# An RWKV-7 core with 16 x 16 inverses, a series of 64 x 64 matmuls and one head on each half of the partitions

## The chip, the core and the metric

The kernel runs on one core of one Trainium2 chip. The metric is the device time of one execution in microseconds (us); lower is better. PE is the matmul engine, PEld its weight loads, DVE the vector engine, ACT the scalar engine, POOL GpSimd, SP the engine that issues the DMAs.

## What is computed

A trunk of two layers on 512 tokens of 1024 channels, in float32. Each layer normalises x, projects it, runs four groups of heads in parallel (a bidirectional Mamba-2 SSD, a bidirectional RWKV-7, differential attention, grouped attention), multiplies the joined outputs by w_out, normalises and adds to x. The change is in the RWKV-7 part. Its core is this scan, for 8 heads of 64 channels and for each of two directions:

```
def step(S, inp):
    r_t, w_t, k_t, v_t, a_t, b_t = inp
    sa = jnp.einsum("bhvk,bhk->bhv", S, a_t)
    S = S * w_t[:, :, None, :] + sa[..., None] * b_t[:, :, None, :] + v_t[..., None] * k_t[:, :, None, :]
    return S, jnp.einsum("bhvk,bhk->bhv", S, r_t)
```

S is a 64 x 64 state. Around it stand token shifts, low-rank decays, a group norm, a bonus term and a gate.

## The kernel before, in words

The scan is computed in chunks of 64 tokens, 8 chunks per direction d, for four pairs j of heads (e is the head in the pair). That makes 32 units (d, e, chunk) per pair. `rwkv` (line 252) runs for each pair:

- **prep** (322): all that needs no product of two tokens. It is done for pair j + 1 while pair j is in work, in small steps that `Ahead` (485) hands out.
- **products** (429) and **turned** (443): b and k against a and r of each chunk (tile AT, through PSUM tile pa), and b, k and v turned so that tokens stand on partitions (BKT; v goes into the upper half of UV).
- **the solver** (519 to 543): each unit needs the inverse of a 64 x 64 unit triangular matrix. DVE turns its two 32 x 32 diagonal blocks to one matrix per partition, on 64 partitions, and inverts them by 31 steps of forward substitution, a multiplication (541, tile ot) and an addition (543, written under the name UV) per step.
- **the merge** (544 to 564): three DVE transposes, 64 matmuls of 32 x 32 (tile pr) for the blocks off the diagonal, and copies into TT, the transposed inverses.
- **the chain** (566 to 618): for 8 chunks in turn, for both directions: products of the state and v (bk, shown as ch), copy to Xs (588), times TT, two copies into UV (591), times BKT, four operations for the new state (606 or 609), and the outputs (tile yb). POOL makes the decayed state Sl (598).

`Filler` (1072) weaves the projections of the next pair (pjc) and the attention (pjt, sc, ptp, ob and others) in between: `fill(F_SV)` after a solver step or `fill(F_CH)` after a chunk releases that many us of its work, scaled so that all of END * 299.5 us is released over the four pairs. A weight is loaded by DMA, split by ACT into a rounded part whi (143) and by POOL into the rest wlo (144), and each product is three matmuls. The framework then orders the instructions of each engine by its own priorities, and every engine works its list in order.

Of the kernel before, what the change touches and what calls it, by code (L numbers as in the profile page):

```python
# [10 lines left out]
F32 = mybir.dt.float32  # L11
F32R = mybir.dt.float32r
# [25 lines left out]
N_SV = 2  # L38
N_CH = 2
C_LAG = 2  # L40
# [6 lines left out]
# columns of the constant array  # L47
# [5 lines left out]
C_BK = C_ONE + 2  # L53
# [4 lines left out]
C_N = C_NHALF + 16  # L58
# kept apart: the masks and chunk starts of the SSD, the rotary tables (cos and sin; 1-D and row positions by token tile)
# [3 lines left out]
# rounded to float32r on the chip, which changes none of them  # L63
# [3 lines left out]
C_ALL = C_E + 16  # L67
# [9 lines left out]
def trunk(ctx: ExitStack, tc: tile.TileContext, x_in, win, wwd, wdt, wout, w2a, cols, rows, sscal, consts, out, dbg=None,  # L77
# [14 lines left out]
    # the activation table comes in while the first loads run  # L92
# [17 lines left out]
    bkcol = cst[:, C_BK:C_BK + 1]  # L110
    nhalf = cst[:, C_NHALF:C_NHALF + 16]
    cr = cpool.tile([128, 272], F32R, name="cr")
# [36 lines left out]
    def pre_norm(xt, tt, lay, pool, pspool, tag):  # L149
        """RMSNorm of one 128-token tile and its transposed, split copy."""  # L150
# [14 lines left out]
    def load_layer(i):  # L165
# [7 lines left out]
        # 1 - mu, w0/2, a0/2, k_a/2, 1 - k_a/2  # L173
# [12 lines left out]
    def proj_cm(i, g, ps, consume):  # L186
        """Two 128-column tiles of the projection, channels on partitions."""
# [14 lines left out]
    def low_rank(pw, ws, tt):  # L202
        """The RWKV's low-rank inputs of two token tiles, channels on partitions."""
# [10 lines left out]
    def proj_early(i, g, ps, consume):  # L214
        """256 columns of the projection, one token tile after another."""
# [16 lines left out]
    def proj_tm(i, g, ps, consume):  # L232
        """256 columns of the projection, tokens on partitions; two token tiles to a bank."""
# [17 lines left out]
    # ------------------------------------------------------------------ RWKV-7  # L251
    def rwkv(i, lay, pw, ps, rp, fill):
        c, dv = lay["cols"], lay["dv"]

        def lerp(raw, n, d, dst):
            """raw + (neighbour - raw) * mu; the backward direction runs in reversed time."""
# [22 lines left out]
        def block_mm(o, m, src):  # L279
            """m @ src for a matrix that float32r holds exactly."""  # L280
# [7 lines left out]
        # states of the two heads of a pair, each in its own block  # L288
        Sbuf = [[rp.tile([128, 2, 64], F32, tag=f"S{d}{n}", name=f"S{d}{n}") for n in range(2)] for d in range(2)]
        for d in range(2):  # L290
            for n in range(2):
                G.memset(Sbuf[d][n], 0.0)

        # a of the pair in work, r of two pairs
        AR = rp.tile([128, 3, 2, 8, 64], F32, tag="AR", name="AR")
# [26 lines left out]
        def prep(j):  # L322
            """Everything of a head pair that needs no product of two of its tokens; yields now and then."""
# [5 lines left out]
            s["a"], s["r"] = Aa, Ar = AR[:, 0], AR[:, 1 + j % 2]  # L329
# [11 lines left out]
            for d in range(2):  # L341
# [19 lines left out]
                # max(sum, 1e-24) as relu(sum - 1e-24) + 1e-24  # L361
# [21 lines left out]
                BK = rp.tile([128, 8, 2, 64], F32, tag="BK", name="BK", bufs=2)  # L383
                s["BK"].append(BK)
# [9 lines left out]
                V.tensor_tensor(BK[:, :, 0, :], v3(b1), il, op=ALU.mult)  # L394
# [33 lines left out]

        def products(j, c0, n):
            """n chunks of AT."""  # L430
            ar = AR[:, 0:2 + j % 2:1 + j % 2]
            for d in range(2):
                BK = sts[j]["BK"][d]
                for e in range(2):
                    hp = slice(64 * e, 64 * e + 64)
                    pa = ps.tile([128, n, 128], F32, tag="g", name="pa")
                    for cc in range(n):
                        mm(pa[:, cc, :].rearrange("p (a t) -> p a t", a=2), BK[hp, c0 + cc].rearrange("p a t -> p (a t)"),
                           ar[hp, :, d, c0 + cc, :], True, True)
                    V.tensor_tensor(AT[:, d, e, c0:c0 + n].rearrange("p c a t -> p c (a t)"), pa,  # L440
                                    rmask.unsqueeze(1).to_broadcast([128, n, 128]), op=ALU.mult)

        def turned(j):
            BK, v = sts[j]["BK"], sts[j]["v"]
            for d in range(2):
                for e in range(2):
# [956 lines left out]
```

## Time and profile before

| | |
|---|---|
| median of 3 runs | 1897.48 us (1895.22 to 1897.68) |
| span of the profiled execution, the one time that the profile gives of it | 1898.5 us |
| busy share of PE / PEld / DVE / ACT / POOL | 89% / 71% / 72% / 44% / 41% |
| four head pairs of layer 1, from the first solver to the last chain | 117.4 to 703.8 us |
| the same of layer 2 | 1056.4 to 1648.9 us |

Busy is the time in which an engine has an instruction in work; matmuls overlap, so a busy PE is not a PE at its peak. PEclk in a row of windows is the granted share of the 2.4 GHz clock, at each moment 1.0 or 0.5 (1.2 GHz). A wait names who waits, for whom, the total, how often and the longest.

### The profile page before, as it was taken

To read this page: it belongs to the slowest core of one execution; us is meant where nothing else is said; L and a number is where in the kernel's file an instruction comes from. 1 tells how busy PE (TensorE), PEld (TensorE's weight loads), DVE (VectorE), ACT (ScalarE), POOL (GpSimd) and SP (SyncE) were. 2 spreads that over 40 slices of the span, in tenths; PEclk is the share of its full clock that TensorE was granted. 3 is DMA by queue.
4 is the path that set the end of the run, shared out by engine and by line. 5 is a ranking of instruction groups with operands and counts; after the bars stand their busy time and mean duration, and the time that the engine had idled before them with its cause. 6 is when DMAs were issued, how large, how long until landed. Compare 5 with 4: busy or idle time off the path is not lost.

```text
span 1898.5 us, 28978 instructions
## 1 busy us (share of the span) xinstructions
PE 1683.3 (89%) x10744; PEld 1340.6 (71%) x10744; DVE 1363.0 (72%) x2946; ACT 838.4 (44%) x1606; POOL 782.7 (41%) x826
## 2 busy tenths in 40 slices
PE   7898988897988898988898899889989888989888
PEld 6576776676776776876775777666767767767666
DVE  4577789779868657886246877887797795588752
ACT  4643345435525245443345442553454252455432
POOL 4433445424542334443455333443444433344433
PEclk9877899898989899989998778998988898999899
DMA  4211111011111114223431111110111111142223
GB/s 147 58 39 43 28 29 51 32 34 40 40 40 30 33 40 137 70 68 93 129 105 49 38 28 32 34 45 31 34 45 28 40 34 35 34 134 62 89 78 117
DMA packets 57485, 107.91 MB, mean 57 GB/s; under 512 B 6784, under 2 KB 8832, under 8 KB 57344
## 3 DMA queue, kind: packets, MB, share of 16 engines
q1 hardware_dynamic: 57344, 106.07, 18.7%
q8 instruction: 84, 1.38, 0.3%
q14 instruction: 57, 0.47, 0.1%
HBM read 95.56 MB, written 10.49 MB: 56 GB/s over the span
## 4 chain that ended last, share of the span: by engine, by line
PE 46%; DVE 36%; POOL 6%; ACT 6%; issue 5%; DMA 2%; POOLq 0%; SPq 0%; ACTq 0%; DVEq 0%
PE pjt L83 9%; PE mix L83 6%; PE pjc L83 5%; PE ch L83 5%; DVE UV L543 5%; DVE ot L541 4%; PE pa L83 4%; PE yb L83 3%; PE sc L83 3%; PE p L83 2%; PE ob L83 2%; POOL wlo L144 2%; DVE As L528 2%; DVE nm L845 1%; PE pr L83 1%
## 5 line engine op out<-in xcount | busy, mean ns | idle before, releaser
L144 POOL TENSOR_TENSOR wlo<-wf,whi 128x512 fp32r<-128x512 f32 x228 | 338.9, 1492 | 334.1 <-ACT whi L143 293.3
L83 PE MATMUL pjt<-whi,hhi 128*128 128x256 f32 x960 | 297.8, 311 | 13.3 <-DVE gate L315 6.9
L83 PE MATMUL pjt<-wlo,hhi 128*128 128x256 f32 x960 | 295.4, 309 | 8.4 <-POOL wlo L144 8.4
L83 PE MATMUL pjt<-whi,hlo 128*128 128x256 f32 x960 | 294.6, 307 | 0.0
L143 ACT ACTIVATE whi<-wf 128x512 fp32r<-128x512 f32 x228 | 141.2, 627 | 226.9 <-PE pjt L83 109.0
L83 PEld LDWEIGHTS pjt<-whi,hhi 128*128 128x128 f32 x960 | 196.1, 204 | 29.9 <-issue 8.1
L83 PEld LDWEIGHTS pjt<-wlo,hhi 128*128 128x128 f32 x960 | 195.4, 204 | 17.3 <-POOL wlo L144 9.0
L83 PEld LDWEIGHTS pjt<-whi,hlo 128*128 128x128 f32 x960 | 195.7, 204 | 8.9 <-issue 5.3
L83 PE MATMUL pjc<-hhi,whi 128*128 128x512 f32 x384 | 165.0, 431 | 11.5 <-ACT raw L269 5.2
L83 PE MATMUL pjc<-hhi,wlo 128*128 128x512 f32 x384 | 163.6, 427 | 0.0
L83 PE MATMUL pjc<-hlo,whi 128*128 128x512 f32 x384 | 162.4, 423 | 0.0
L598 POOL TENSOR_SCALAR Sl<-S,lamC,cst 128x128 f32<-128x128 f32 x96 | 47.1, 491 | 248.0 <-DVE S L606 168.1
L83 PE MATMUL sc<-qT,qT 64*128 64x512 f32 (+1 forms) x256 | 108.3, 519 | 21.6 <-ACT p L848 11.6
L541 DVE TENSOR_TENSOR ot<-As,UV 64x31 f32<-64x31 f32 (+15 forms) x248 | 123.7, 499 | 5.0
L543 DVE TENSOR_TENSOR UV<-UV,ot 64x31 f32<-64x31 f32 (+15 forms) x248 | 121.3, 489 | 5.2
L848 ACT ACTIVATE p<-sc,nm 128x512 f32<-128x512 f32 x96 | 65.7, 685 | 108.0 <-DVE nm L845 107.7
L83 PE MATMUL mix<-whi,ylo 128*128 128x512 f32 x256 | 106.1, 414 | 5.5 <-DVE ylo L1189 5.5
L83 PE MATMUL mix<-wlo,yhi 128*128 128x512 f32 x256 | 104.6, 409 | 0.0
L83 PEld LDWEIGHTS pjc<-hhi,whi 128*128 128x128 f32 x384 | 77.9, 203 | 33.9 <-ACT raw L269 6.8
L83 PE MATMUL mix<-whi,yhi 128*128 128x512 f32 x256 | 99.7, 411 | 1.9 <-ACT yhi L1188 1.9
L606 DVE SCALAR_TENSOR_TENSOR UV<-ch,lamC,Sl 64x64 f32<-64x64 f32 x192 | 54.0, 281 | 58.7 <-PE ch L83 35.4
L845 DVE TENSOR_REDUCE nm<-sc 128x1 f32<-128x512 f32 x96 | 65.6, 683 | 38.4 <-PE sc L83 37.7
(316 smaller groups left out, 4013.0 us busy)
## 6 DMA issues: line engine op xcount, KB each, us to landing
wf<-in_win_dram SPq DMA_DIRECT2D x224, 256.0 KB, 2.9
wf<-in_wout_dram SPq DMA_DIRECT2D x64, 256.0 KB, 2.6
y<-y_dram SPq DMA_DIRECT2D x24, 256.0 KB, 3.2
xt<-in_x_dram SPq DMA_DIRECT2D x8, 512.0 KB, 4.0
y_dram<-y SPq DMA_DIRECT2D x16, 256.0 KB, 2.0
y_dram<-rs SPq DMA_DIRECT2D x8, 256.0 KB, 2.8
x_dram<-t SPq DMA_DIRECT2D x8, 256.0 KB, 2.2
xt<-x_dram SPq DMA_DIRECT2D x4, 512.0 KB, 3.7
```

The lines of the kernel that those rows point to most:

```text
L83: PE.matmul(o, lhsT, rhs, start=start, stop=stop, skip_group_check=skip)
L143: S.activation(hi, wf, AF.Copy)
L144: G.tensor_tensor(lo, wf, hi.bitcast(F32), op=ALU.subtract)
L528: V.transpose(out=As[hp], in_=ATu[hp, :, 0, hp].rearrange(swap))
L541: V.tensor_tensor(o3, As[:, jj + 1:32, jj:jj + 1].to_broadcast([64, n, jj + 1]), Ti[:, jj:jj + 1, 0:jj + 1].to_broadcast([64, n, jj + 1]), ...
L543: V.tensor_tensor(Ti[:, jj + 1:32, 0:jj + 1], Ti[:, jj + 1:32, 0:jj + 1], o3, op=ALU.add)
L598: G.tensor_scalar(Sl, St[d], lamC[:, d, cc:cc + 1], zero, op0=ALU.mult, op1=ALU.add)
L606: V.scalar_tensor_tensor(dst, bk[hp, 128:192], lc, Sl[hp, e, :], op0=ALU.mult, op1=ALU.add)
L845: V.tensor_reduce(nm, sc, axis=AX, op=ALU.max, negate=True)
L848: S.activation(p, sc, AF.Exp, bias=nm, accum_out=sm)
```

## The change

- The diagonal blocks are 16 x 16. DVE turns all four quarters of the partitions, folds the two halves of each 32 x 32 transpose into one matrix per partition on 128 partitions, and needs 15 steps instead of 31. Eight transposes write the inverses back, as DN and, transposed, DT.
- The rest of each 64 x 64 inverse comes from a series: Mp is the part off the diagonal blocks times DN, and three rounds compute TT = DT + Mp TT by matmuls (PSUM tiles ch). POOL masks the blocks and clears DT and DN.
- Head e stands on partitions 64 e to 64 e + 63. Almost every matmul of the core is 64 x 64, one for each head, on that half of the rows and of the columns. A pair has 464 of them (before 218 of other shapes); each shows as two PE instructions, as before.
- Products with v leave the chain: px, pk and py are made for all chunks at once, and the bank yb and py are first written by a matmul with a zero weight. The chain has three matmul steps per chunk with a DVE operation behind each; the decayed state is one DVE operation instead of one of POOL, and the new state one instead of four.
- `fill` is called 15 + 5 + 24 times per pair instead of 31 + 1 + 8, with other amounts; a is kept for two pairs.

```diff
 F_P0 = 0.92
-F_SV = 0.83
-F_MG = 1.44
-F_CH = 3.72
+F_SV = 1.5
+F_MG = 2.4
+F_CH = 1.7
...
-N_SV = 2
-N_CH = 2
-C_LAG = 2
+C_LAG = 4
...
-        AR = rp.tile([128, 3, 2, 8, 64], F32, tag="AR", name="AR")
+        AR = rp.tile([128, 4, 2, 8, 64], F32, tag="AR", name="AR")
...
         def products(j, c0, n):
...
-                for e in range(2):
-                    hp = slice(64 * e, 64 * e + 64)
-                    pa = ps.tile([128, n, 128], F32, tag="g", name="pa")
-                    for cc in range(n):
-                        mm(pa[:, cc, :].rearrange("p (a t) -> p a t", a=2), BK[hp, c0 + cc].rearrange("p a t -> p (a t)"),
-                           ar[hp, :, d, c0 + cc, :], True, True)
+                pa = [ps.tile([128, n, 128], F32, tag="g", name="pa") for _ in range(2)]
+                for cc in range(n):
+                    for m in range(2):
+                        for e in range(2):
+                            mm(pa[m][half[e ^ m], cc, :].rearrange("p (a t) -> p a t", a=2), BK[half[e], c0 + cc, m, :],
+                               ar[half[e], :, d, c0 + cc, :], True, True)
...
-        fill.scale = END * 299.5 / (4 * (31 * F_SV + 2 * F_MG + 8 * F_CH) + F_GN)
+        fill.scale = END * 299.5 / (4 * (15 * F_SV + 5 * F_MG + 24 * F_CH) + F_GN)
...
-            As = rp.tile([64, 32, 32], F32, tag="b4", name="As", bufs=1)
...
+            for q in range(4):
+                V.transpose(out=As[quad[q][0]].rearrange("p t (h s) -> p t h s", h=2), in_=unit(ba, q))
+            V.scalar_tensor_tensor(As2, As[:, :, 0:16], th[0], As[:, :, 16:32], op0=ALU.mult, op1=ALU.add)
...
+            G.tensor_tensor(bam, bam, nomask.unsqueeze(1).to_broadcast([128, 16, 64]), op=ALU.mult)
+            G.memset(DT, 0.0)
+            G.memset(DN, 0.0)
+            for jj in range(15):
+                ahead()
+                fill(F_SV)
+                n = 15 - jj
...
+                V.tensor_tensor(o3, As2[:, jj + 1:16, jj:jj + 1].to_broadcast([128, n, jj + 1]),
+                                Ti[:, jj:jj + 1, 0:jj + 1].to_broadcast([128, n, jj + 1]), op=ALU.mult)
+                V.tensor_tensor(Ti[:, jj + 1:16, 0:jj + 1], Ti[:, jj + 1:16, 0:jj + 1], o3, op=ALU.add)
...
-            for jj in range(31):
-                if jj % N_SV == 0:
-                    ahead()
-                fill(F_SV)
-                n = 31 - jj
...
+            for q in range(4):
+                V.transpose(out=unit(DN, q), in_=Dx[quad[q][0]].rearrange("p t h s -> p s h t"))
+            for q in range(4):
+                V.transpose(out=unit(DT, q), in_=Dx[quad[q][0]])
...
             for d in range(2):
...
+                pm = chd(d)
+                for cc, e in both:
+                    mm(pm[half[e], cc, :], ba[half[e], d, cc, :], DN[half[e], d, cc, :], True, True)
+                S.activation(Mp[:, d], pm, AF.Copy)
+            TT = rp.tile([128, 2, 8, 64], F32, tag="dn", name="TT", bufs=1)
+            for n in range(3):
+                ahead()
+                fill(F_MG)
+                for d in range(2):
+                    ph = chd(d)
+                    for cc, e in both:
+                        mm(ph[half[e], cc, :], Mp[half[e], d, cc, :], (TT if n else DT)[half[e], d, cc, :], True, True)
+                    V.tensor_tensor(TT[:, d], ph, DT[:, d], op=ALU.add)
...
+            for d in range(2):
+                px = ps.tile([128, 8, 64], F32, tag="g", name="px")
+                for cc, e in both:
+                    mm(px[half[e], cc, :], AT[1][half[1 - e], d, cc, 0, :], V2[half[1 - e], d, cc, :], True, True)
+                S.activation(ba[:, d], px, AF.Copy)
...
-                for e in range(2):
-                    mm(yb[64 * e:64 * e + 64, d, cc % 4, :], UV[:, d, e, cc, :], AT[:, d, e, cc, 1, :], cc == 0, True,
...
-                    mm(bk[:, 64:128], TT[:, d, cc].rearrange("p e t -> p (e t)"), Xs, True, True)
...
                 for d in range(2):
-                    bk = ps.tile([128, 192], F32, tag=f"ch{d}", name=f"ch{d}")
+                    bk = bks[d]
...
+                        Xs = rp.tile([128, 64], F32, tag=f"Xs{d}", name=f"Xs{d}", bufs=1)
+                        V.tensor_tensor(Xs, bk[:, 0, :], ba[:, d, cc, :], op=ALU.add)
                     for e in range(2):
...
+                        mm(bk[half[e], 1, :], TT[half[e], d, cc, :], Xs[half[e]], True, True)
+                ahead()
+                fill(F_CH)
+                for d in range(2):
+                    bk = bks[d]
+                    if 0 < cc < 7:
+                        Sl = rp.tile([128, 64], F32, tag=f"Sl{d}", name=f"Sl{d}", bufs=1)
+                        V.scalar_tensor_tensor(Sl, St[d], lamC[:, d, cc:cc + 1], KV[:, d, cc, :], op0=ALU.mult, op1=ALU.add)
+                    Us = rp.tile([128, 64], F32, tag=f"Us{d}", name=f"Us{d}", bufs=1)
+                    V.tensor_copy(Us, bk[:, 1, :])
+                    if cc < 7:
+                        for e in range(2):
+                            mm(bk[half[e], 2, :], BKT[half[e], d, e, cc, :], Us[half[e]], True, True)
+                        Sn = rp.tile([128, 64], F32, tag=f"S{d}", name=f"S{d}", bufs=2)
+                        V.scalar_tensor_tensor(Sn, bk[:, 2, :], lamC[:, d, cc:cc + 1], Sl if cc else KV[:, d, 0, :],
+                                               op0=ALU.mult, op1=ALU.add)
```

DVE, the first pair of layer 1, late in the solver. In these rows lr, lk, rn and lam belong to prep. Before:

```order
L543 TENSOR_TENSOR UV<-UV,ot 64x14x18
L381 TENSOR_TENSOR AR<-lr,lam 128x512
L541 TENSOR_TENSOR ot<-As,UV 64x247
L380 SCALAR_TENSOR_TENSOR rn<-lk,cols,rn 128x512
L543 TENSOR_TENSOR UV<-UV,ot 64x13x19
L388 TENSOR_TENSOR lk<-ka,lk 128x512
L541 TENSOR_TENSOR ot<-As,UV 64x240
L391 TENSOR_TENSOR AR<-rn,lam 128x512
L543 TENSOR_TENSOR UV<-UV,ot 64x12x20
L393 SCALAR_TENSOR_TENSOR b_1296<-tha,rn 128x512
L541 TENSOR_TENSOR ot<-As,UV 64x231
```

After, the last steps of the solver, the start of the transposes and the first work of prep:

```order
L541 TENSOR_TENSOR ot<-sv 128x39
L543 TENSOR_TENSOR sv<-sv,ot 128x3x13
L541 TENSOR_TENSOR ot<-sv 128x28
L543 TENSOR_TENSOR sv<-sv,ot 128x2x14
L541 TENSOR_TENSOR ot<-sv 128x15
L543 TENSOR_TENSOR sv<-sv,ot 128x15
L547 TENSOR_SCALAR sv<-sv,cst 128x16x16 x2
L549 STREAM_TRANSPOSE DN<-sv 32x16x2x16 x2
L347 TENSOR_SCALAR thw<-thw 128x512
L261 SCALAR_TENSOR_TENSOR lr<-raw,cols,lt 128x512
L353 SCALAR_TENSOR_TENSOR cs<-cst,thw 128x128 x4
L549 STREAM_TRANSPOSE DN<-sv 32x16x2x16 x2
```

The work of prep, which stood between the steps of the solver, now stands behind all of them.

PE, the merge of the same pair, before (p are matmuls of prep, pjt and sc those of the attention):

```order
L83 MATMUL pr_1417<-Mb,UV 32x32 x16
L83 MATMUL pr<-Mb,UV 32x32 x16
L83 MATMUL pjt<-whi,hhi 128x256
L83 MATMUL pjt<-whi,hlo 128x256
L83 MATMUL pjt<-wlo,hhi 128x256
L83 MATMUL sc<-qT_1316,qT_1307 128x512
L83 MATMUL sc<-qT_1316,qT_1308 128x512
L83 MATMUL pr_1455<-Mb,UV 32x32 x16
L83 MATMUL p_1484<-low_290,w_1114 128x512
L83 MATMUL ch_1533<-Xs_1536,TT 128x64
L83 MATMUL ch_1549<-Xs_1552,TT 128x64
```

After, the three rounds of the series (the line names the turned inverse DT, then TT):

```order
L82 MATMUL ch_1371<-DT,Mp 64x64 x16
L82 MATMUL ch_1389<-DT,Mp 64x64 x16
L82 MATMUL p_1452<-bh,cr 128x512
L82 MATMUL ch_1416<-TT,Mp 64x64 x16
L82 MATMUL ch_1434<-TT,Mp 64x64 x16
L82 MATMUL p_1452<-bl,cr 128x512
L908 MATMUL pqt<-cst,qk 128x128 x4
L82 MATMUL ch_1480<-TT,Mp 64x64 x16
L82 MATMUL ch_1498<-TT,Mp 64x64 x16
```

The small 32 x 32 matmuls are gone, and in their place stand rows of 16 matmuls for each direction, with few others between the rounds.

## Rows read from the trace of the kernel before

**Rows 1.** Windows, first layer's four head pairs: solver, then merge and chain, of each.
```profile
core 0: us, PE busy (x) PEld busy (x) DVE busy (x) ACT busy (x) POOL busy (x), PEclk, DMA share, GB/s
117.40:167.30 49.90, 42.59 (x251) 34.92 (x249) 47.61 (x92) 28.16 (x49) 22.18 (x19) 0.90 0.18 49
167.30:263.20 95.90, 92.69 (x670) 69.82 (x669) 66.81 (x172) 32.56 (x60) 31.35 (x37) 0.84 0.10 27
263.20:329.00 65.80, 53.10 (x315) 41.75 (x314) 62.96 (x119) 42.77 (x77) 37.01 (x25) 0.95 0.16 43
329.00:413.70 84.70, 78.76 (x624) 58.63 (x622) 60.28 (x159) 27.88 (x52) 28.02 (x37) 0.90 0.11 32
413.70:465.50 51.80, 40.23 (x262) 34.96 (x261) 47.61 (x91) 28.16 (x56) 25.13 (x17) 0.90 0.16 47
465.50:576.30 110.80, 101.90 (x780) 79.83 (x779) 87.34 (x219) 47.66 (x95) 47.52 (x53) 0.91 0.12 34
576.30:616.60 40.30, 34.87 (x234) 28.41 (x233) 37.78 (x81) 25.36 (x54) 11.90 (x10) 0.96 0.12 34
616.60:703.80 87.20, 80.45 (x701) 65.65 (x701) 53.86 (x166) 25.55 (x66) 28.68 (x39) 0.92 0.13 38
sum 586.40, PE 524.58 PEld 413.99 DVE 464.25 ACT 258.12 POOL 231.79; mean PE 65.57 PEld 51.75 DVE 58.03 ACT 32.26 POOL 28.97
```

**Rows 2.** Windows, second layer's four pairs.
```profile
1056.40:1648.90 592.50, 532.48 (x3823) 420.06 (x3822) 464.29 (x1092) 257.97 (x503) 232.56 (x236) 0.89 0.13 36
```

**Rows 3.** Waits of PE in the first layer's four pairs, five rows of 17.
```profile
PE ptp L870 <- DVE p L1005: 9.3, 5, 3.8
PE sc L83 <- ACT p L848: 5.8, 4, 3.6
PE ptp L870 <- ACT p L848: 5.7, 5, 2.2
PE pqt L881 <- DVE qk L904: 5.6, 1, 5.6
PE pjt L83 <- POOL wlo L144: 3.7, 1, 3.7
```

**Rows 4.** Groups of DVE in the first pair, 117.4 to 263.2 us.
```profile
L541 DVE TENSOR_TENSOR ot<-As,UV 64x31 f32<-64x31 f32 (+15 forms) x31 | 15.6, 502 | 0.6
L543 DVE TENSOR_TENSOR UV<-UV,ot 64x31 f32<-64x31 f32 (+15 forms) x31 | 14.2, 459 | 0.7
L591 DVE COPY UV<-ch 64x64 f32<-64x64 f32 x32 | 7.0, 219 | 8.5 <-PE ch L83 7.8
L606 DVE SCALAR_TENSOR_TENSOR S<-ch,lamC,Sl 64x64 f32<-64x64 f32 x24 | 6.8, 283 | 0.5
L606 DVE SCALAR_TENSOR_TENSOR UV<-ch,lamC,Sl 64x64 f32<-64x64 f32 x24 | 6.8, 282 | 9.4 <-PE ch L83 6.6 <-PE yb L83 2.6
```

**Rows 5.** Groups of DVE there, shapes kept apart.
```profile
L541 DVE TENSOR_TENSOR ot<-As,UV 64x60 f32<-64x60 f32 x2 | 0.4, 215 | 0.1
L440 DVE TENSOR_TENSOR AT<-pa,cst 128x512 f32<-128x512 f32 x1 | 0.7, 691 | 1.1 <-PE pa L83 1.1
```

**Rows 6.** Windows of PE by tile, sums over four pairs: ch, yb, pr, pa.
```profile
sum 586.40, PE 70.16; mean PE 17.54
sum 586.40, PE 55.92; mean PE 13.98
sum 586.40, PE 21.38; mean PE 5.34
sum 586.40, PE 33.37; mean PE 8.34
```

**Rows 7.** Timeline of PE, one burst: start us, us, what.
```profile
160.48 0.45 PE L83 MATMUL ch<-UV,AT 64*64 64x64 f32 x8
```

**Rows 8.** Groups of PE, the same burst.
```profile
L83 PE MATMUL ch<-UV,AT 64*64 64x64 f32 x8 | 0.4, 230 | 0.0
```

**Rows 9.** Windows, the stretch that begins in the merge of the first pair.
```profile
171.90:192.30 20.40, 20.40 (x144) 13.80 (x141) 9.93 (x24) 9.21 (x14) 3.58 (x6) 0.50 0.02 8
```

More of the change, by code (lines that the diff above doesn't have):

```diff
@@ L109, in trunk @@
     zero = cst[:, C_ZERO:C_ZERO + 1]
-    bkcol = cst[:, C_BK:C_BK + 1]
+    nomask = cst[:, C_NOM:C_NOM + 64]
+    th = [cst[:, C_TH + n:C_TH + n + 1] for n in range(2)]
     nhalf = cst[:, C_NHALF:C_NHALF + 16]
-    cr = cpool.tile([128, 272], F32R, name="cr")
+    cr = cpool.tile([128, 288], F32R, name="cr")
     cen2, mean2, selE = cr[:, 0:128], cr[:, 128:256], cr[:, 256:272]
@@ new lines, in rwkv @@
+            G.memset(sv[:, 768:1024], 0.0)
+            G.memset(sv[:, 768:1024:17], 1.0)
+            quad = [(slice(32 * q, 32 * q + 32), slice(32 * (q % 2), 32 * (q % 2) + 32)) for q in range(4)]
+            unit = lambda t, q: t[quad[q][0], :, :, quad[q][1]].rearrange("p d c (h t) -> p t h (d c)", h=2)
+            for q in range(4):
+                V.transpose(out=As[quad[q][0]].rearrange("p t (h s) -> p t h s", h=2), in_=unit(ba, q))
+            V.scalar_tensor_tensor(As2, As[:, :, 0:16], th[0], As[:, :, 16:32], op0=ALU.mult, op1=ALU.add)
@@ new lines, in rwkv @@
+            both = [(cc, e) for cc in range(8) for e in range(2)]
+            Mp = rp.tile([128, 2, 8, 64], F32, tag="sv", name="Mp", bufs=1)
+            for d in range(2):
+                pm = chd(d)
[5 more added lines that the diff above has]
+                ahead()
+                fill(F_MG)
+                for d in range(2):
[3 more added lines that the diff above has]
+                    V.tensor_tensor(TT[:, d], ph, DT[:, d], op=ALU.add)
@@ new lines, in rwkv @@
+            ahead()
+            fill(F_MG)
+            KV = rp.tile([128, 2, 8, 64], F32, tag="sv", name="KV", bufs=1)
+            Y0 = rp.tile([128, L], F32, tag="dt", name="Y0", bufs=1)
+            for d in range(2):
[3 more added lines that the diff above has]
+                S.activation(ba[:, d], px, AF.Copy)
+            for d in range(2):
+                pk = ps.tile([128, 8, 64], F32, tag="g", name="pk")
+                for cc, e in both[:14]:
+                    mm(pk[half[e], cc, :], BKT[half[1 - e], d, e, cc + e, :], V2[half[1 - e], d, cc, :], True, True)
+                V.tensor_tensor(KV[:, d, 0:7], pk[:, 0:7, :], lamC[:, d, 0:7].unsqueeze(2).to_broadcast([128, 7, 64]),
+                                op=ALU.mult)
@@ new lines, in rwkv @@
+            py = ps.tile([128, L], F32, tag="g", name="py")
+            clear = lambda o: mm(o, cr[:, 272:273].to_broadcast([128, 128]), hT["hi"][:, 0, :], True, True)
+            rev = lambda d, cc: slice((7 * d + (1 - 2 * d) * cc) * 64, (7 * d + (1 - 2 * d) * cc) * 64 + 64)
+            clear(py)
+            for d in range(2):
+                for cc, e in both:
+                    mm(py[half[e], rev(d, cc)], V2[half[1 - e], d, cc, :], AT[1][half[1 - e], d, cc, 1, ::1 - 2 * d],
+                       False, True, True)
@@ L568, in rwkv @@
+            S.activation(Y0, py, AF.Copy)
+            made = 0
+            yb = ps.tile([128, L], F32, tag="yb", name="yb")
+            clear(yb)
             St = [None, None]
[L569 removed]
             for cc in range(8):
[L571 to L573 removed]
+                if cc >= C_LAG:
                     ahead.finish()
@@ L578, in rwkv @@
                     made += n
+                bks = []
+                for d in range(2):
+                    bk = ps.tile([128, 8, 64], F32, tag=f"ch{d}", name=f"bk{d}")
+                    bks.append(bk)
+                    if cc:
+                        for e in range(2):
+                            mm(bk[half[e], 0, :], Aa[half[e], d, cc, :], St[d][half[e], :], True, True)
+                ahead()
                 fill(F_CH)
-                if cc % 4 == 0:
-                    yb = ps.tile([128, 2, 4, 64], F32, tag="yb", name="yb")
@@ L1296, in _consts @@
     m = np.where(p[None, :] < 64, strict, incl).astype(np.float32)
-    c[:, C_RMASK:C_RMASK + 128] = m * np.where(p[:, None] < 64, -0.5, 1.0)
+    c[:, C_RMASK:C_RMASK + 128] = m
+    c[:, C_NOM:C_NOM + 64] = (s[:, None] // 16 < np.arange(64)[None, :] // 16)
+    for n in range(2):
+        c[:, C_TH + n] = (p % 32 // 16 == n)
     c[:, C_MNEG:C_MNEG + 128] = np.where(p[:, None] <= p[None, :], 0.0, -1e30)
@@ L1320, in _consts @@
     c[:, C_ONE] = 1.0
-    c[:, C_BK] = np.where(p < 64, -0.5, 1.0)
     c[:, C_GNEPS] = GN_EPS
```

156 lines of the change are left out of this document (52 added, 104 removed).

## The prediction, made before the changed kernel was run

> **What bounds the kernel now.** I read the windows first, because a busy share over the whole span averages stages with different limits. In the four pairs of layer 1 two kinds of stretch alternate [rows 1]. In the four solver stretches VectorE (DVE) is busy 47.61 of 49.9, 62.96 of 65.8, 47.61 of 51.8 and 37.78 of 40.3 us, so it sets the pace there, and TensorE (PE) stands idle for 7.3, 12.7, 11.6 and 5.4 us. In the merge and chain behind them PE sets the pace (92.69 of 95.9 us, 78.76 of 84.7) and DVE has room (66.81 and 60.28). Layer 2 is the same to 2% [rows 2]. So there are three things to gain: PE's idle time, the time that its clock takes, and its own work.
>
> - Idle: 586.40 - 524.58 = 61.8 us in layer 1 and 592.5 - 532.48 = 60.0 in layer 2, together **121.8 us**.
> - Clock: PE's busy time by one minus the granted clock, window by window, is 50.7 us in layer 1 [rows 1] and 532.48 x 0.11 = 58.6 in layer 2 [rows 2], together **109 us**.
> - The rest, some 950 us, is PE at work at full clock.
>
> The waits of PE tell who leaves it idle [rows 3]. Five of the 17 rows, the four longest and the longest behind POOL, sum to 30.1 us. ptp and pqt wait for DVE directly (9.3 and 5.6); sc and ptp wait for ACT's p (5.8 and 5.7), which itself needs DVE's maxima and comes late when DVE is late. So 26.4 of the 30.1 go back to DVE, 88%, and 3.7 to POOL's split of a weight. These are not waits of the RWKV core but of the attention woven into it: DVE serves it late because it is in the solver.
>
> **The change, part by part, for one of the eight pairs.**
>
> *DVE, solver.* 31 multiplications and 31 additions cost 15.6 + 14.2 = 29.8 us [rows 4]. Now there are 30 operations of at most 64 elements per partition. The nearest row is 64x60, 0.215 us [rows 5]: 6.5 us. The upper end is the old means of 0.50 and 0.46: 14.4. I take 6.5, since the sizes agree and only the number of partitions differs. The transposes carry as many elements as before (six of 1024, now twelve of 512): nothing, at most twelve times 0.215 = 2.6 more. **-23.3.**
>
> *DVE, chain.* Gone are 32 copies (7.0) and 48 of the state operations (6.8 + 6.8) [rows 4]. In their place stand 16 Us at 0.22 and 12 Sl and 14 Sn at 0.283: 10.9. The operation behind Xs was there before as a copy. **-9.7.**
>
> *DVE, new.* Six additions for TT and two for KV, of 128x512 or a little less, at the 0.691 of AT from PSUM [rows 5]: 5.5. Three operations around the solver, of 128 x 256, about 1. **+6.6.** In sum 26.4 us of DVE's 464.25 / 4 = 116 per pair go, 211 over the eight.
>
> *PE.* Before, ch, yb and pr take 17.54 + 13.98 + 5.34 per pair, and pa 33.37 / 3 = 11.1 in each of the three pairs that have it [rows 6]: 48.0 us, at a clock near 0.90, or 43.2 at full clock. What a 64 x 64 matmul costs now I read from one burst: eight instructions take 0.45 us [rows 7] and one by itself 0.230 [rows 8], so each further one adds (0.45 - 0.23) / 7 = 0.031. The series, px, pk, py and the turned v are 504 instructions in long rows: 15.6. The chain has 296 in short bursts, counted as 37 bursts of eight: 16.6. Products are 128 with twice the columns, at 0.063: 8.1. The two clears are four with eight times the columns: 1.0. Together 41.3. The difference of 2 lies within what the counting can do, and I take **0**, with -10 to +6 per pair as the ends.
>
> *POOL and ACT.* Sl and the copies of TT and AT leave POOL; a mask and four fills come. POOL is busy 231.79 of 586.40 us and ACT 258.12 [rows 1], and the new POOL work lies beside the solver's 15 steps: 0. If that cover fails, the DVE transposes into DN wait; the price is of the size of POOL's longest wait in PE's list, 3.7 [rows 3], 30 us over eight. No DMA is added or moved, so SP and the queues stay out of the sum.
>
> *Order.* Filler hands out by shares. Before, solver, merge and chain got 31 x 0.83, 2 x 1.44 and 8 x 3.72: 44, 5 and 51%. Now it is 15 x 1.5, 5 x 2.4 and 24 x 1.7: 30, 16 and 54%. As the order shows, the last solver steps follow each other without prep between them, and prep stands behind them; PE meanwhile has its list of projections. The series' rounds stand almost bare on PE. That costs little: a round of 32 instructions for one direction (1.0 us) covers the 0.69 us addition of the other. The chain's steps wait for DVE 22 times per direction, and 24 fills stand in between; what is late next is an addition of 0.28 us, no longer four operations in line.
>
> **The sum.** Of the idle 121.8 us, 88% or 107 go back to DVE. DVE loses 26.4 of its 116 us per pair, but some of its lateness is prep and norms that stay, so I take two thirds: **-71** (ends 0 and -107). Of the clock, one stretch at 0.50 of the clock (1.2 GHz) begins among the pr matmuls of the first merge and lasts 20.4 us [rows 9], so 10.2 us are lost. Those matmuls go. Were every merge like that, 82 of the 109 us would come back; rows of 64 x 64 matmuls stand in their place, though, so I take a third: **-36** (ends -80, and +40 if the new rows hold the clock down as the old ones did and longer). PE's own work 0, POOL 0. Together -107: 1898.5 - 107 = 1791 us. The profiled execution's span lies 1.0 us above the median of the runs, so it stands for them: **1791 us**.
>
> **Rivals.**
>
> *A. The two halves take turns (slower).* Matmuls of the two heads alternate, each on its half of PE's rows, into the two halves of the partitions of one PSUM bank. No row of before shows two row halves in work at once: the burst that gave 0.031 [rows 7, 8] keeps to one half of the rows and alternates the columns. If a matmul has to wait for the other half, each instruction adds twice as much: 504 x 0.031 + 128 x 0.063 + 296 x 0.031 = 32.9 us per pair, 263 over eight: 1791 + 263 = 2054. It decides from the point where that eats the 107, at 41% of it: a spacing above 0.044 us instead of 0.031. For it: it would hit nearly every new matmul. Against: the two column halves do overlap in that burst, into one bank, and here too the outputs lie on different partitions. Chance 0.11.
>
> The Trainium skill, page "TensorEngine Tiling (Array Packing)", section "Gotcha 1: PSUM Pressure", speaks against this change: different row tiles cannot use one PSUM bank at the same time, and the software has to keep them apart. By that rule the time would be rival A's 2054; no row of before shows it. The Trainium skill, page "PSUM — Partial Sum Buffer", section "PSUM bank collisions raise a hardware error", narrows this by a measurement of its own to one bank and the same quarter of the partitions, which the two heads never share; by that one 1791 stands.
>
> *B. The freed time becomes waits for weights.* With DVE early, PE reaches each projection sooner, and pjt waits for wlo, as it does once already for 3.7 us [rows 3]. Then of the idle time only some 25 us come back and of the clock 10: 1863. For it: POOL works wlo off in order behind other work. Against: POOL is 40% busy. Chance 0.15.
>
> *C. The clock falls over the new rows.* The 504 instructions in long rows are 15.6 us per pair and 125 over eight at full clock, and at a granted clock of 0.5 as much again. If that happens to half of them, the time is 1791 + 63 = 1854; if to all, 1916, and the point from which this is slower is 107 of 125, six sevenths of them. For it: [rows 9]; against: the pr matmuls go, and PE has fewer gaps. Chance 0.05.
>
> *D. More comes back.* All idle time that hangs on DVE (-107) and 80 of the clock: 1711. Chance 0.07.
>
> **How the numbers follow.** The forecast case has 0.62; by its ends it reaches from 1725 (-107 idle, -66 clock) to 1845. Of the cases, A and D lie outside the range, B and the mild form of C inside if it goes up to 1880; down I go to 1720. That leaves out some 0.2. Slower is A alone and the worst of C: 0.12. A measurement of this kernel can tell 0.2%, 3.8 us, from no change; that the cases meet there by chance: 0.03. Faster: 0.85.
>
> **What would show it.** Right: the solver's two DVE lines near 0.2 us each and 6 to 7 us per pair; DVE no longer above 90% in any solver stretch; PE's waits for p and qk shorter; instructions of the rows of ch, px, pk and py 0.03 us apart; the pairs 45 to 60 us shorter per layer, the rest of the span unchanged. Wrong: a spacing of 0.06 (A), waits of pjt for wlo at the head of PE's list (B), a clock near 0.5 where the series runs (C). If PE's idle time falls by more than 107 us, its waits were DVE's to a greater part than the five rows say.

## The result and the profile after

The changed kernel takes 1853.64 us (median of 4 runs, 1847.4 to 1858.17) where the kernel before took 1897.58 beside it. The ratio is 0.975 [0.9712, 0.9787]: faster, as forecast, but by 44 us and not by 107. The profiled execution spans 1852.6 us, 45.9 less than that of before.

The windows of the kernel after, by stage (four pairs of layer 1, SSD to the next layer's prep, four pairs of layer 2, the end), answer to [rows 1, 2]:

```profile
core 0: us, PE busy (x) PEld busy (x) DVE busy (x) ACT busy (x) POOL busy (x), PEclk, DMA share, GB/s
113.50:674.00 560.50, 502.92 (x5615) 404.83 (x5614) 365.15 (x829) 240.63 (x474) 187.90 (x184) 0.94 0.12 37
674.00:1033.20 359.20, 317.05 (x1743) 257.29 (x1743) 217.01 (x387) 164.21 (x309) 161.39 (x178) 0.95 0.28 90
1033.20:1593.00 559.80, 502.87 (x5576) 405.52 (x5570) 364.18 (x827) 240.55 (x475) 187.87 (x184) 0.93 0.12 37
1593.00:1852.60 259.60, 229.36 (x1161) 185.88 (x1159) 158.43 (x312) 108.22 (x218) 106.38 (x115) 0.94 0.28 91
```

Of the kernel before, the two stages that the prediction left out of its sum:

```profile
703.80:1056.40 352.60, 312.87 (x1553) 253.59 (x1551) 216.78 (x381) 160.56 (x301) 159.40 (x175) 0.91 0.29 89
1648.90:1898.50 249.60, 219.73 (x1093) 177.60 (x1092) 158.81 (x309) 104.95 (x211) 104.29 (x112) 0.95 0.29 92
```

The pairs fall from 1178.9 to 1120.3 us, by 25.9 in layer 1 and 32.7 in layer 2, where 45 to 60 each were forecast. By the books of the prediction, in these windows: PE's idle time is 57.6 + 56.9 = 114.5 (before 121.8), the clock takes 502.92 x 0.06 + 502.87 x 0.07 = 65.4 (109), and PE's work at full clock is the rest, 940.4 (947.8). So **idle -7, clock -44, work -7**. The clock column is rounded to 0.01, up to 2.5 us per layer; the same stretches read in windows of 2 us give the clock 110.3 before and 60.6 after, so nearer to -50, and -2 for the work. The SSD stages give 6.6 + 10.0 back, since more of the attention is left for them (68 more PE instructions in the last one), and the first stage is 3.9 shorter: -45.9.

DVE's groups in the first pair answer to [rows 4, 5]:

```profile
L549 DVE STREAM_TRANSPOSE DN<-sv 32x512 f32<-32x512 f32 x4 | 4.8, 1198 | 0.1
L543 DVE TENSOR_TENSOR sv<-sv,ot 128x15 f32<-128x15 f32 (+7 forms) x15 | 4.2, 279 | 0.5
L571 DVE TENSOR_TENSOR TT<-ch,DT 128x512 f32<-128x512 f32 x6 | 4.1, 685 | 1.1 <-PE ch L82 0.9
L541 DVE TENSOR_TENSOR ot<-sv 128x15 f32<-128x15 f32 (+7 forms) x15 | 4.1, 271 | 0.5
L635 DVE COPY Us<-bk 128x64 f32<-128x64 f32 x16 | 3.0, 216 | 4.6 <-PE bk L82 4.6
L529 DVE SCALAR_TENSOR_TENSOR sv<-sv,cst 128x256 f32<-128x256 f32 x1 | 2.7, 2740 | 0.0
```

The solver's two lines are 8.3 us, where 29.8 stood. DVE's busy time over the whole execution falls from 1363.0 to 1163.1 us, by 200; forecast were 211. The kernel before:

```profile
PE 1683.3 (89%) x10744; PEld 1340.6 (71%) x10744; DVE 1363.0 (72%) x2946; ACT 838.4 (44%) x1606; POOL 782.7 (41%) x826
```

So DVE did what was forecast, and PE's idle time did not follow. PE's waits in layer 1 answer to [rows 3]:

```profile
PE p L82 <- ACT bh L283: 12.8, 3, 10.9
PE bk L82 <- DVE Xs L624: 8.4, 2, 4.5
PE ptp L897 <- DVE p L1032: 6.9, 6, 2.1
PE ptp L897 <- DVE ot L541: 3.9, 1, 3.9
PE bk L82 <- DVE S L640: 3.6, 3, 1.8
PE p L82 <- POOL bl L284: 3.4, 3, 1.8
PE pqt L908 <- DVE qT L913: 3.0, 1, 3.0
```

The waits of the attention (sc, ptp, pqt) are shorter, but prep (p) and the chain (bk) now wait instead. The longest, 10.9 us, occurs once per layer, in the first pair:

```profile
137.85 1.85 PE L82 MATMUL ch<-DN,AT 64*64 64x64 f32 x56 [1.69 <-DVE DN L549]
150.64 0.80 PE L82 MATMUL p<-bh,cr 128*128 128x512 f32 x1 [10.94 <-ACT bh L283]
151.37 0.69 PE L82 MATMUL ch<-DN,AT 64*64 64x64 f32 x6
```

While PE stands there, DVE's list holds this (some rows left out):

```profile
135.44 2.36 DVE L549 STREAM_TRANSPOSE DN<-sv 32x512 f32<-32x512 f32 x2
137.83 4.30 DVE L551 STREAM_TRANSPOSE DT<-sv 32x512 f32<-32x512 f32 x4
142.16 0.69 DVE L375 TENSOR_TENSOR AR<-lr,lam 128x512 f32<-128x512 f32 x1
...
148.18 1.75 DVE L400 SCALAR_TENSOR_TENSOR rk<-lr,cols,lk 128x512 f32<-128x512 f32 x1
```

The p of line 82 needs rk, which ACT rounds to bh. DVE makes rk at 148.18 us, behind the eight transposes and six operations of prep. PE does its list in order, so the last six instructions that make Mp (ch<-DN), and with them the series, stand behind p.

### The profile page after: what moved, and what is told of

The parts are those of the page before. It is cut to its first block, busy times and chain, and to the rows that moved or that the text cites. A ratio compares the mean times of both kernels' runs of the same rounds, so it can differ in the third digit from the quotient of the medians.

```text
span 1852.6 us, 35939 instructions
## 1 busy us (share of the span) xinstructions
PE 1642.2 (89%) x14616; PEld 1325.0 (72%) x14616; DVE 1163.1 (63%) x2426; ACT 810.5 (44%) x1566; POOL 698.9 (38%) x728
## 5 line engine op out<-in xcount | busy, mean ns | idle before, releaser
L144 POOL TENSOR_TENSOR wlo<-wf,whi 128x512 fp32r<-128x512 f32 x228 | 315.6, 1389 | 444.7 <-ACT whi L143 360.2
L82 PE MATMUL pjt<-whi,hlo 128*128 128x256 f32 x960 | 287.9, 300 | 0.0
L143 ACT ACTIVATE whi<-wf 128x512 fp32r<-128x512 f32 x228 | 141.3, 628 | 215.8 <-PE pjt L82 104.0
L82 PE MATMUL pjc<-hhi,wlo 128*128 128x512 f32 x384 | 159.7, 418 | 0.0
L82 PE MATMUL pjc<-hlo,whi 128*128 128x512 f32 x384 | 158.1, 412 | 0.0
L82 PE MATMUL sc<-qT,qT 64*128 64x512 f32 (+1 forms) x256 | 101.7, 494 | 7.2 <-ACT y L1055 3.8
L82 PEld LDWEIGHTS pjc<-hhi,wlo 128*128 128x128 f32 x384 | 76.3, 199 | 21.4 <-issue 4.2
L82 PEld LDWEIGHTS pjc<-hlo,whi 128*128 128x128 f32 x384 | 76.5, 199 | 15.7 <-issue 0.3
L1224 POOL TENSOR_TENSOR wlo<-wf,whi 128x512 fp32r<-128x512 f32 x32 | 44.4, 1390 | 112.3 <-ACT whi L1223 107.6
L1223 ACT ACTIVATE whi<-wf 128x512 fp32r<-128x512 f32 x64 | 40.4, 631 | 94.0 <-PE mix L82 59.3
```

The costliest lines, as they stand in the source:

```text
L82: PE.matmul(o, lhsT, rhs, start=start, stop=stop, skip_group_check=skip)
L1224: (V if kt % 2 else G).tensor_tensor(lo, wf, hi.bitcast(F32), op=ALU.subtract)
```

## The experiments

**One wait, and DVE's amount.** hold6 moves the prep step:

```diff
-                ahead()
+                if j or jj >= 6:
+                    ahead()
                 fill(F_SV)
```

> The changed kernel, but in the first pair of each layer the first six solver steps hand out no prep, so that the prep matmul for which PE waits 10.9 us in the merge stands later in PE's list. Theory 'place' (the idle time did not go because PE's list now stands waiting at one wrong place): the wait of 10.9 us goes in both layers, and the 13.7 and 17.1 us of half clock behind it; 2 x 10.9 + 0.5 x 30.8 = 37 us, so 1853.6 - 37 = 1817 (1808 to 1830). Rival 'amount' (the idle time follows how much DVE has to do, which is unchanged here): the wait only moves, 1849 to 1858.

Measured: 1857.04 us (1848.19 to 1862.89), ratio 0.9738 [0.9686, 0.9789]. The wait for bh is gone from the first pair, and others stand there now:

```profile
PE ch L82 <- DVE DN L550: 6.9, 2, 3.9
PE pa L82 <- DVE AT L433: 2.4, 1, 2.4
PE sc L82 <- DVE qT L914: 1.7, 1, 1.7
```

In the second pair PE has 12.7 us of idle time where the changed kernel has 9.3 (149.80 - 137.14 and 143.70 - 134.37):

```profile
241.60:391.40 149.80, 137.14 (x1471) 110.41 (x1470) 101.64 (x213) 69.96 (x126) 52.97 (x54) 0.92 0.13 39
```

```profile
244.20:387.90 143.70, 134.37 (x1437) 105.00 (x1438) 98.59 (x217) 70.02 (x127) 53.43 (x53) 0.98 0.13 41
```

Over the four pairs of layer 1 PE is idle for 57.8 us (567.60 - 509.78), where it was 57.6. A single wait is not where the time hangs. Theory "place" falls. The next run was made with the kernel of hold6 as it stands, its solver steps left in, so it tells nothing of its own question; as a repeat (1862.25 us) it tells that 5 us between such runs mean little.

> As hold6, and the 15 solver steps are left out (30 DVE operations of 0.21 us, 6.5 us per pair, 52 us in all; the inverses of the diagonal blocks are then not computed). Rival 'amount', with the rate of the prediction (107 us for 211 us of DVE, 0.51): 26 us below hold6. Theory 'place': what is left of DVE's time in the solver is mostly beside PE, 0 to 10 us below hold6.

hold6_more4 adds DVE work in each solver step (more4 and more8 do the same on the changed kernel, with 4 and 8):

```diff
+                for _ in range(4):
+                    V.tensor_tensor(od, As2[:, 0:8, 0:8], As2[:, 8:16, 0:8], op=ALU.mult)
```

> As hold6, and four more DVE operations of 0.22 us on a scratch tile in each of the 15 solver steps: 60 per pair, 13 us per pair, 104 us in all. Rival 'amount' (0.51): 53 us above hold6. Theory 'place': the work of the solver comes later, but PE has other rows in its list: 10 to 30 us above hold6.

Measured: 1855.39 us, no more than hold6. Both theories missed. So the price of DVE's time was measured over a longer stretch:

> The changed kernel without the 15 solver steps (30 DVE operations of 0.21 us, 6.5 us per pair, 52 us in all; the inverses of the diagonal blocks are not computed). 'Amount' (PE's idle time follows DVE's work, 0.51 us per us as in the prediction): 1853.6 - 26 = 1828 (1820 to 1836). 'Beside' (DVE's work in the solver lies beside a list of PE that is long enough, as 104 us more of it cost nothing in hold6_more4): 1846 to 1860.

> The changed kernel with four more DVE operations of 0.22 us in each solver step (13 us per pair, 103 in all): the middle between the changed kernel and more8, which took 47 us more for 206. If DVE's time has one price, 23 us more, ratio 0.987; if the first 100 us lie beside PE's list, as hold6_more4 has it, under 8 us more, ratio 0.975 to 0.979.

> The changed kernel with eight more DVE operations of 0.22 us on a scratch tile in each solver step: 120 per pair, 26 us per pair, 206 in all, so that DVE is as busy as in the kernel before. 'Amount': what the change gave by way of DVE is taken back, 0.51 x 206 = 105 us, 1958 (1930 to 1975). 'Beside': 1850 to 1875.

Measured: nosteps 1843.86 us, more4 1851.52, more8 1900.97 (1897.68 to 1905.6, ratio 0.9979 [0.9948, 1.0009]). By "amount" all three are wrong; by "beside" nosteps and more4 come out a little faster than its ranges, and more8 slower. First rows of the page of the changed kernel, nosteps, more4 and more8, in this order:

```profile
PE 1642.2 (89%) x14616; PEld 1325.0 (72%) x14616; DVE 1163.1 (63%) x2426; ACT 810.5 (44%) x1566; POOL 698.9 (38%) x728
```

```profile
PE 1638.2 (89%) x14616; PEld 1324.5 (72%) x14616; DVE 1122.4 (61%) x2186; ACT 809.7 (44%) x1566; POOL 698.6 (38%) x728
```

```profile
PE 1640.2 (89%) x14616; PEld 1322.4 (71%) x14616; DVE 1229.2 (66%) x2906; ACT 812.1 (44%) x1566; POOL 696.9 (38%) x728
```

```profile
PE 1658.3 (87%) x14616; PEld 1339.9 (71%) x14616; DVE 1343.6 (71%) x3386; ACT 810.9 (43%) x1566; POOL 691.7 (36%) x728
```

The added operations are shorter than expected, so DVE's own totals count: 1122, 1163, 1229 and 1344 us. The first 66 us above the changed kernel cost nothing, the next 114 cost 49 (0.43 each), and 41 below it give 10 (the four were not all on one chip, and some 5 us lie between repeats; nosteps and more8, on one chip, are 57 us apart for 221 us of DVE). **The price is not one rate: nothing over the 66 us above the changed kernel, and steep where DVE comes near its old amount.** The windows of more8's pairs:

```profile
112.00:696.60 584.60, 509.97 (x5614) 411.99 (x5611) 455.64 (x1309) 241.12 (x474) 184.22 (x184) 0.92 0.11 36
1055.60:1643.50 587.90, 514.24 (x5614) 414.77 (x5615) 455.97 (x1309) 240.81 (x474) 184.65 (x184) 0.92 0.11 35
```

With DVE at 456 us per layer (before 464), PE is idle for 74.6 + 73.7 = 148.3 us, 26.5 more than before; the clock takes 81.9, 27 less. From more8 to the changed kernel, that is for the 180 us of scratch work, idle time falls by 34 and the clock by 17 (81.9 - 65.4). But more8 is not the new order alone: its scratch work (od) stands in the solver, in front of the attention, and makes waits of its own. The longest of PE in layer 1:

```profile
PE ptp L900 <- DVE od L546: 11.0, 4, 3.7
PE pjt L82 <- DVE gate L309: 10.2, 2, 9.3
PE bk L82 <- DVE Xs L627: 9.0, 3, 4.5
```

In layer 2 the first of them is 12.5 us. So of the 26.5 us up to 23.5 may come from where the scratch work stands, and how much the order adds by itself is not shown.

bhalf makes the solver saving alone, in the kernel before:

```diff
+                if jj % 2:
+                    continue
                 V.tensor_tensor(o3, As[:, jj + 1:32, jj:jj + 1].to_broadcast([64, n, jj + 1]),
```

> The kernel before, with every second of the 31 solver steps left out (15 steps, 0.50 + 0.46 us each, 14.4 us of DVE per pair, 115 in all; the inverses are then wrong). The solver saving alone, nothing else of the change. 'Amount': 0.51 x 115 = 59 us less, 1840 (1825 to 1855) where the kernel before has 1898 to 1904. 'Beside': within 15 us of the kernel before.

Measured: 1887.12 us (1867.22 to 1889.69) beside 1904.44, ratio 0.9889 [0.9813, 0.9964], with DVE 94 us less busy (1268.7): 0.18 us per us. PE's idle time in its pairs is 115.7 us (1163.1 - 1047.48), 6 less than before. "Amount" with 0.51 is refuted there too, and "beside" is missed by 2 us.

**The two halves, and the clock.** emajor orders the long rows by head:

```diff
-            both = [(cc, e) for cc in range(8) for e in range(2)]
+            both = [(cc, e) for e in range(2) for cc in range(8)]
```

> The changed kernel with the 440 PE instructions per pair of the long rows (series, px, pk, py) written for all chunks of head 0 first and then of head 1, so that neighbours are on the same half of the rows and columns. In the trace of the changed kernel, with the heads in turn, 56 of them take 1.85 us, 0.030 us apart. Theory 'halves' (two neighbours overlap because they are on different halves): 0.06 us apart, 440 x 0.03 = 13 us more per pair, 80 to 105 us in all: 1935 to 1960. Rival (an instruction follows the one before at 0.03 us wherever it stands): no change, 1849 to 1858.

Measured: 1924.03 us, ratio 1.0097 [1.0061, 1.0133]. The timeline of one row of px at full clock, in the changed kernel and then in emajor:

```profile
313.64 2.08 PE L82 MATMUL px<-V,AT 64*64 64x64 f32 x64
```

```profile
644.88 3.01 PE L82 MATMUL px<-V,AT 64*64 64x64 f32 x58
```

By one's 0.22 us: (2.08 - 0.22) / 63 = 0.030 us with the heads in turn, (3.01 - 0.22) / 57 = 0.049 with one head behind the other. With the heads in turn the recorded starts of this row come in pairs, 0.007 us apart, with 0.052 to the next pair: neighbours on different halves do overlap, in one PSUM bank. (They differ in rows and in columns; the burst of [rows 7], which alternates the columns alone, had 0.031 too, so which of the two it takes is not shown.) "Halves" holds, with 0.049 instead of its 0.06: 440 x 8 x 0.019 = 67 of the 70 us. The wait of 10.9 us in the first pair is the same in both kernels. The half clock that begins within it is not (changed kernel, then emajor):

```profile
143.20:156.80 13.60, 6.16 (x50) 3.67 (x51) 10.17 (x12) 6.59 (x11) 9.01 (x9) 0.50 0.18 58
```

```profile
139.20:180.10 40.90, 30.34 (x241) 26.54 (x242) 21.93 (x29) 13.41 (x21) 10.06 (x13) 0.50 0.09 27
```

The granted clock is 0.50, that is 1.2 GHz, for 13.6 us in one and for 40.9 in the other, where PE works at the same matmuls one half at a time. In layer 2 it is 17.1 and 37.5, and in a repeat of the changed kernel (again, below) 20.5 and 13.6. Whether it is the halves or the longer rows as such was not separated.

bnopr replaces the small matmuls of the merge, in the kernel before:

```diff
-                for u, uu in enumerate(units):
-                    mm(pr[:, u, :], W1[32:64, uu, :], Mb[32:64, uu, :], True, True)
+                for d in range(2):
+                    u0 = d * 16 + e * 8
+                    mm(pr[:, 8 * d:8 * d + 8, :], W1[32:64, u0, :], Mb[32:64, u0:u0 + 8, :], True, True)
```

> The kernel before, with the 64 matmuls of 32 x 32 in each merge (pr) replaced by 8 of 32 x 256 that write the same PSUM columns (one weight for eight units: the off-diagonal blocks are then wrong). 'Rows of small matmuls pull the clock down': of the 358 us at half clock in the profiled execution before, 85 begin in or right behind pr; without them 43 us less, about 1857 (1845 to 1870). Rival 'gaps' (the clock falls behind PE's gaps, which stay): 1885 to 1904.

Measured: 1871.15 to 1906.26 us (clocks 0.908 to 0.883), ratio to the kernel before 0.9888 [0.9777, 0.9999]. The times are inconclusive. The profile, of the run of 1871.15 us, says more: the half clock of the first merge ([rows 9], 20.4 us) is there without the small matmuls too:

```profile
168.60:185.60 17.00, 16.83 (x59) 8.81 (x57) 9.10 (x19) 6.78 (x13) 1.18 (x2) 0.50 0.01 1
```

Read in windows of 2 us the clock takes 119 us in its pairs (before 110). What is less there is PE's work, by 25 us. That 43 us of clock hang on pr is not borne out.

**Does another order find the missing time?** Each of these was made from the changed kernel. gqk50e hands out a run of 12 DVE operations, which stands in front of Xs, in parts:

```diff
-END = 0.98
+END = 1.113
...
             for tt in range(4):
                 for h in range(3):
...
+                yield 5.0
```

> The changed kernel, with the run of 12 DVE operations (5.5 us, normalising the grouped attention's q and k) handed out in four parts, and END raised from 0.98 to 1.113 so that the pairs still get the same share of the attention. In the trace of the changed kernel PE waits 4.5 and 3.9 us in each layer for Xs, which stands behind this run in DVE's list, and the clock is halved for 27 us behind the four waits. Theory 'runs' (PE's idle time hangs on single runs of DVE work ahead of a step, not on DVE's total): the four waits shrink below 1.5 us each, 17 + 13 = 30 us, ratio to the kernel before 0.975 - 0.016 = 0.959 (0.955 to 0.968). Rival 'fixed' (a wait that goes comes back at another place, as in hold6): 0.970 to 0.980.

Measured: 1883.76 us, ratio 0.9863 [0.9788, 0.9938], slower than both theories had it. The four waits for Xs do shrink, to 0.7 us in each layer, but PE's idle time in the pairs is 133.5 us (1152.2 - 1018.67) where it was 114.5, with waits at ptp, sc and pa. The pairs hold as much work as before (5628 PE instructions in a layer, before 5615), so this is the order and not a larger share. The share alone is changed by END:

```diff
-END = 0.98
+END = 1.047
```

> The changed kernel with END at 1.047 instead of 0.98, so that 20 us more of the attention are given out within the four pairs of a layer. In the changed kernel the two SSD stages took 15 us longer than before, because work went from the pairs to them. If that work is cheaper inside the pairs: ratio 0.968 to 0.973. If it costs the same at either place: 0.973 to 0.979.

Measured: 1885.12 us, ratio 0.9871, outside both ranges: the work costs more inside the pairs.

> The changed kernel with END at 0.92 instead of 0.98: 18 us less of the attention given out in the four pairs of each layer. 'Amount' (work in the pairs costs twice what it costs in the SSD stages, as end1047 measured): pairs 32 us shorter per layer, SSD 16 longer, ratio 0.975 - 0.017 = 0.958 (0.955 to 0.968). 'Core' (the pairs have a fixed idle time, and 0.98 is past what they take): 0.970 to 0.980.

Measured: 1870.83 us, ratio 0.9816. With 0.86:

> The same with END at 0.86, 36 us less in the pairs of each layer. 'Amount': below end92. 'Core': PE's list runs out in the pairs, its idle time there rises above 57 us per layer, ratio 0.975 to 0.990.

Measured: 1876.43 us, ratio 0.985. The windows of the pairs, sums of end1047 and of end92:

```profile
sum 1188.30, PE 1063.15 PEld 856.09 DVE 741.26 ACT 503.77 POOL 389.11; mean PE 531.57 PEld 428.05 DVE 370.63 ACT 251.88 POOL 194.56
```

```profile
sum 1085.20, PE 970.88 PEld 785.87 DVE 722.45 ACT 468.13 POOL 366.30; mean PE 485.44 PEld 392.93 DVE 361.23 ACT 234.06 POOL 183.15
```

At END 1.047 the pairs take 68 us more than the 1120.3 of the changed kernel and the SSD stages 38 less; at 0.92 the pairs take 35 less, and the SSD stages 52 more. In end92 PE's idle time in the pairs is 114.3 us, what it is in the changed kernel (114.5): "amount" falls, and "core" has the idle time right, though not the ratio. At 0.86 it is the other way round: the ratio lies in the range of "core", but the idle time is 108.3 us (1059.3 - 950.99) and did not rise, so its mechanism is not shown.

gpipe gives PE the grouped attention's scores one step ahead:

```diff
                     p, r, _ = softmax_rows(sc, ap)
                     yield 0.9
-                    V.tensor_scalar(r, r, 0.5, None, op0=ALU.mult)
-                    ob = pT_av(p, vs[u], qb, ps, ap)
-                    S.activation(y[:, qb, :], ob, AF.Copy, scale=r[:, 0:1])
-                    yield 1.3
+                    if pend:
+                        done(*pend)
+                        yield 1.3
+                    pend = (p, r, y, qb)
```

> The changed kernel, with the grouped attention one step ahead: the scores of the next 128 tokens are given to PE before the transposition (ptp) of the last ones. In the changed kernel ptp waits for p for some 13 us per layer, a third of it in this part. Theory 'distance' (PE's list puts a step too close behind the DVE and ACT work that it needs): 4 to 8 us per layer less, ratio 0.968 to 0.973. Rival 'fixed': 0.973 to 0.979.

Measured: 1845.59 us, ratio 0.9663 [0.96, 0.9727]. The two together:

> gpipe (0.966 with END at 0.98) with END at 0.92. If the two act on different waits: ratio 0.008 below end92. If on the same ones: as the better of the two alone.

Measured: 1882.27 us, ratio 0.987, above both; they are not independent. Then gpipe beside the changed kernel on one chip:

> The changed kernel as it is, on the same chip as gpipe_b: 1849 to 1858, ratio 0.970 to 0.978.

> gpipe as before (the grouped attention's scores one step ahead). If its gain is real: 6 to 10 us below again. If it was the chip: within 3 us of it.

Measured: again 1849.30 us, gpipe_b 1849.00. What looked like a gain lay between chips.

> The changed kernel, with the multiplication that masks the diagonal blocks (POOL, 2.4 us per pair, beside the first solver steps) done by DVE. If DVE's slow operations there are slow because POOL works beside them: the 128x256 operation falls from 2.07 to about 0.4 us and the first step from 1.18 to 0.18, against 1.4 us of new work. As DVE's time has no price at this amount: within 5 us of again.

```diff
-            G.tensor_tensor(bam, bam, nomask.unsqueeze(1).to_broadcast([128, 16, 64]), op=ALU.mult)
+            V.tensor_tensor(bam, bam, nomask.unsqueeze(1).to_broadcast([128, 16, 64]), op=ALU.mult)
```

Measured: 1843.77 us (1839.21 to 1846.3), 5.5 below again, just outside what was expected. DVE's groups of maskdve in the first pair:

```profile
L532 DVE TENSOR_TENSOR AT<-AT,cst 128x1024 f32<-128x1024 f32 x1 | 1.2, 1219 | 0.0
L529 DVE SCALAR_TENSOR_TENSOR sv<-sv,cst 128x256 f32<-128x256 f32 x1 | 0.5, 484 | 0.0
```

The 128x256 operation falls from 2740 to 484 ns. Beside POOL's mask it had been stretched more than fivefold; the first solver step falls to 0.17 us. Of the versions that compute the same this has the lowest median here, 0.3% below the changed kernel on the same chip (1846.51 to 1855.11 us).

## Why the prediction was right in part, and where it was wrong

- **DVE's terms held.** Forecast 211 us less, measured 200. The solver took 8.3 us in the first pair and not 6.5, and the 128x256 operation ahead of it 2.7, since POOL works beside them; POOL was put at 0, and its mask cost DVE 2.3 us there (2.74 against 0.48 without it). The timelines of POOL and of DVE show that both end together, within 0.3 us:

```profile
117.89 2.41 POOL L532 TENSOR_TENSOR AT<-AT,cst 128x1024 f32<-128x1024 f32 x1 [7.67 <-DVE sv L528]
120.43 1.31 POOL L144 TENSOR_TENSOR wlo<-wf,whi 128x512 fp32r<-128x512 f32 x1
```

```profile
117.84 2.74 DVE L529 SCALAR_TENSOR_TENSOR sv<-sv,cst 128x256 f32<-128x256 f32 x1
120.62 1.15 DVE L541 TENSOR_TENSOR ot<-sv 128x15 f32<-128x15 f32 x1
```

  The Trainium skill, page "SBUF — State Buffer", section "🔬 SBUF: two separate sides", has a lock that a DVE operation with two SBUF inputs and a GpSimd operation take in turns, for a whole instruction. The ends in these rows and maskdve agree with it; who began first the rows don't show, as the starts are 0.05 us apart.
- **PE's own work held**: 0 forecast, -2 to -7 in the pairs, with attention work handed to the SSD stages, which take some 17 us longer. The sum did not have that. The spacing in the long rows is 0.030 (forecast 0.031).
- **The clock's term was near by luck** (-36 forecast, -44 to -50 in the pairs): its reason does not hold, as bnopr has the half clock of the first merge without pr's small matmuls. Some 17 of it lie between more8 and the changed kernel and go with DVE's amount; what gave the rest stays open. What the runs show besides is that the order of the long rows changes how long the clock stays at half around one and the same wait (emajor).
- **The step that failed is the sum's first: "Of the idle 121.8 us, 88% or 107 go back to DVE ... so I take two thirds: -71."** It was -7. It took the share of waits whose releaser is DVE as a rate for DVE's time, 0.51 us of the total per us of DVE with the clock. The runs show other prices: 0.18 in the kernel before, for the 94 us that bhalf saves in the solver; in the rebuilt one 0.43 for the 114 us below more8's 1344 and nothing for the next 66. Between more8 and the changed kernel DVE's amount was worth 34 us of idle time and 17 of clock; by bhalf's 0.18 the 200 us would be worth some 36 in all. Either way it is half of what the sum had, or less.
- **The second error is "That costs little"**, said of the new order. In the new order the longest waits stand at p (10.9 us), Xs and ptp, behind runs of DVE work. At nearly DVE's old amount (more8) the rebuilt core has 26.5 us more idle time in the pairs than the kernel before, but part of that stands behind the scratch work itself. So that the order took back what DVE's saving gave is argued and not shown; which of the new places costs how much was not separated, and hold6 shows why: a wait that is taken away there is made up in the same pair and the next.
- **Rival A fell.** Its rule, from the Trainium skill, page "TensorEngine Tiling (Array Packing)", section "Gotcha 1: PSUM Pressure", that different row tiles cannot use one PSUM bank at the same time, does not cost time here: two matmuls on different halves begin 0.007 us apart in one bank, 0.030 us on the mean, against 0.049 on the same half. Where page and measurement differ, the measurement decides; here the two halves also lie on different partitions of the bank. **Rival B fell** too: wlo is not among PE's waits in the pairs. **C** is there in small: 13.6 us at half clock in layer 1 and 17.1 in layer 2 reach from the wait into the series, and PE is busy for 6.16 us of the 13.6.

What stays open is what holds the last 114 us of idle time in the pairs. Neither less DVE work, nor one wait, nor less attention took more than some 10 us of it away; the least with the heads in turn is 105.3, in maskdve (1107.2 - 1001.89).

## What to carry to other kernels

The name of a releaser in the waits tells who came last, not what a us less of that engine is worth. Measure the price before counting on it: add scratch work to the engine in two sizes and leave some out, three cheap kernels, and see where the curve is flat. Look at the waits of these kernels too: scratch work delays what stands behind it, and that is not what the old work delayed. In a kernel whose engines work fixed lists in order, an engine's saving is worth something only as far as it was late, and a changed order brings waits of its own.

## What was not expected

- Around the same wait of 10.9 us, the clock stayed at half for 13.6 us (17.1 in layer 2) with the heads in turn and for 40.9 (37.5) with one head behind the other.
- 66 us more of DVE work in the solvers cost nothing (more4 1851.52 us), 180 cost all that the change had given (more8 1900.97).
- A DVE operation of 128x256 took 2740 ns beside a POOL multiplication of 2.41 us, and 484 without it.
- Some 20 us of attention given to the pairs made the kernel 31 us slower, and as much taken from them 17 (on other chips than the 1853.64 us; by the ratios 23 and 13).
